# Gated one-hots in a top-k expert layer: one VectorE multiply per four tokens, or eight ScalarE copies with a per-partition scale

## The chip, the cores and the metric

The kernel runs on one core of one Trainium2 chip. The metric is device microseconds (us) of one execution, from the median of several runs. The engines are named as the profile names them: PE is TensorE (with PEld, its weight load), DVE is VectorE, ACT is ScalarE, POOL is GpSimd and SP is SyncE.

## What is computed

A two-layer network over 512 tokens of width 1024: a state-space mixer in layer 0, sliding-window attention in layer 1, and after each a "PEER" expert layer, which is where the change lies. Cut to what matters:

```python
def peer_ffn(x, norm_g, q_w, sub_keys, u, v):          # T = 512 tokens, 8 heads, 16 experts per head
    h = rmsnorm(x, norm_g).reshape(T, D)
    ...                                                # scores of 2 x 128 sub-keys, two top-16 lists,
    idx = jnp.take_along_axis(cand_i, best_pos, axis=-1)   # expert = i1 * 128 + i2, 16384 experts
    gate = jax.nn.softmax(best_s, axis=-1).astype(x.dtype)
    def block(inp):
        hb, ib, gb = inp
        a = jnp.einsum('nd,nhkd->nhk', hb, u[ib])
        w = gb * jax.nn.gelu(a, approximate=False)
        return jnp.einsum('nhk,nhkd->nd', w, v[ib])
```

## The kernel before

The first 128 tokens fetch their 128 expert rows each by indirect DMA (`gather_step`, L669). The other 384 tokens take another way: all 16384 experts are computed densely, and the gates are scattered into a dense matrix G of 16384 gates per token. G is made by matmuls of one-hots. For a token, the 128 chosen (head, rank) pairs lie on the partitions; `o[:, q, 0]` is the one-hot of i1, `o[:, q, 1]` that of i2, and `og` is the first one-hot times the gate. The gate is kept in two fp16 parts, a high one and the remainder, so `og` has two rows of 128 per token, and G of a token is the sum of two 128x128 matmuls of `o[:, q, 1]` with the parts of `og`.

**The stage.** In `peer` (L640) the loop over 128 blocks of experts (L982) does this in each step j: `lin` (L206) issues 24 matmuls, each 128x128 weights by 384 tokens, three for each of eight slices (L202 to L204); `next_w` (L154) has put a weight block's split ahead of it, ACT's `whi` copy (L169) and POOL's `wlo` subtraction in four quarters (L172), two blocks ahead; ACT takes the result through Gelu into `ga` (L993) and issues its store (L994); `gather(URATE)` (L995) does 1.17 steps of the gather on average, a DVE multiply (L678) and an indirect DMA (L695) each; and `self.step(BRATE)` (L996) takes background work out of a list.

**The order of the background work.** `bg` (L912) writes the list out by hand: a top-k of a head (T) costs 6.0, the decoding of the indices and gates of 128 tokens (D) some 11 in four items, a block of four tokens of G (G_) costs 1.5. A step adds 2.65 to a credit and takes items while the credit is above zero, so a step takes two blocks of G_ or one, and none for some steps after a T. Each block b is `onehot(b)` (L878) and, one item later, `gmm(b)` (L889): its eight matmuls (L898), the copy of the result to `gsz` by ACT (L899) and, after every fourth block, a store from ACT's queue (L902). Since `gmm` comes one item later, a step with two blocks issues in this order: `onehot(b)`, `gmm(b-1)`, `onehot(b+1)`, `gmm(b)`. All engines work in the order of issue.

```python
                    for b in range(32 * tt + lo, 32 * tt + hi):
                        items.append((1.5, lambda b=b: one(b)))
```

There are 96 blocks in each of the two layers. Tile buffers: `o` (its tile is named `early`) has 3, `og` 2, the score banks 2. The gates come to their place in `turn` (L861), once for each of three groups of 128 tokens: three PE transposes into a bank, then copies by ACT and DVE into `iT` (indices) and `gT` (gates), each value twice side by side so that DVE can read pairs.

Of the kernel before, what the change touches and what calls it, by code (L numbers as in the profile page):

```python
# [11 lines left out]
F32 = _mybir.dt.float32  # L12
# [4 lines left out]
AF = _mybir.ActivationFunctionType  # L17
OP = _mybir.AluOpType
AX = _mybir.AxisListType

P = 128
# [8 lines left out]
ND = NT - NG  # L30
# [4 lines left out]
QT = 4  # L35
GSCALE = 32768.0
F16 = _mybir.dt.float16
# [25 lines left out]
class Net:  # L63
# [54 lines left out]
    def plan(self):  # L118
        t, s = self.t, self.srcs
        w, off = t["wlin"], 0  # L120

        def lin(n):
            nonlocal off
            for _ in range(n):
                s.append(w[off])
                off += 1

        def peer(i):
            lin(16)
            for j in range(NBLK):  # L130
                s.append(t["ut"][i * NBLK + j])
            for j in range(NBLK):
                s.append(t["v"][i * NBLK + j])

        lin(66)
        peer(0)
        lin(8 + 21)
        peer(1)
        lin(8)
# [500 lines left out]
    def peer(self, L):  # L640
        nc, t, tc = self.nc, self.t, self.tc
        mm = nc.tensor.matmul
        vt = nc.vector
# [103 lines left out]
        with ExitStack() as ctx:  # L747
            mp = ctx.enter_context(tc.tile_pool(name="pm", bufs=2, reuse_waits="tile"))
            hp = ctx.enter_context(tc.tile_pool(name="ph", bufs=1, reuse_waits="tile"))
# [26 lines left out]
            pos = hp.tile([P, NTT, HEADS, TOPK], U32, name="pos")  # L776
            idx = hp.tile([P, 2, NTT, HEADS, TOPK], U32, name="idx")
            iT = hp.tile([P, ND, 2, 2], F16, name="iT")
            gT = hp.tile([P, ND, 2, 2], F16, name="gT")
            iota = hp.tile([P, P], F16, name="iota")  # L780
            vt.tensor_copy(iota, self.const[:, C_IOTA:C_IOTA + P])
            i16 = hp.tile([P, TOPK, QT], F16, name="i16")
# [30 lines left out]
            def fl(ap):  # L813
                return ap.rearrange("p a b -> p (a b)")
# [31 lines left out]
            def decode_e(tt):  # L846
                gt, fi = dec.pop(tt)
                sm = mp.tile([P, 2, HEADS], F32, name="sm")
                vt.tensor_reduce(sm[:, 0], gt, axis=AX.X, op=OP.add)
                vt.reciprocal(sm[:, 1], sm[:, 0])  # L850
                gk = mp.tile([P, TOPK, HEADS], F32, name="gk", bufs=1)
                vt.tensor_tensor(gk, gt.rearrange("p h k -> p k h"), sm[:, 1, None, :].to_broadcast([P, TOPK, HEADS]),
                                 op=OP.mult)
                if tt == 0:
                    ef = wg[:, 0]
                    vt.tensor_scalar(ef, fi[0], float(P), float(L * NBLK * P), op0=OP.mult, op1=OP.add)
                    vt.tensor_tensor(ef, ef, fi[1], op=OP.add)
                    vt.tensor_copy(eg, ef)
                    vt.tensor_copy(gate, fl(gk))

                def turn():  # L861
                    if tt == 0:
                        self.gi = 0
                        return
                    pt = self.bank(7)
                    for j, src in enumerate(fi + [fl(gk)]):
                        nc.tensor.transpose(pt[:, j * P:(j + 1) * P], src, self.ident)
                    ts = slice(tt * P - NG, (tt + 1) * P - NG)
                    two = lambda j: pt[:, j * P:(j + 1) * P, None].to_broadcast([P, P, 2])
                    for j in range(2):  # L870
                        nc.scalar.activation(iT[:, ts, j], two(j), AF.Copy)
                    nc.scalar.activation(gT[:, ts, 0], two(2), AF.Copy, scale=GSCALE)
                    vt.scalar_tensor_tensor(gT[:, ts, 1], two(2), GSCALE, gT[:, ts, 0], op0=OP.mult, op1=OP.subtract)
                return turn

            gs = {}
# [1 line left out]
            def onehot(b):  # L878
                o = mp.tile([P, QT, 2, P], F16, name="early", bufs=3)
                og = mp.tile([P, QT, 2, P], F16, name="og")  # L880
                ts = slice(QT * b - NG, QT * b - NG + QT)
                pairs = lambda ap: ap.rearrange("p t c (a d) -> p t c a d", d=2)
                alike = lambda ap: ap[:, ts, :, None, :].to_broadcast([P, QT, 2, P // 2, 2])
                vt.tensor_tensor(pairs(o), iota.rearrange("p (a d) -> p a d", d=2)[:, None, None].to_broadcast(  # L884
                    [P, QT, 2, P // 2, 2]), alike(iT), op=OP.is_equal)
                vt.tensor_tensor(pairs(og), pairs(o)[:, :, 0:1].to_broadcast([P, QT, 2, P // 2, 2]), alike(gT), op=OP.mult)  # L886
                return o, og

            def gmm(b, o):  # L889
# [22 lines left out]
            def bg():  # L912
# [12 lines left out]
                def G_(tt, lo, hi):  # L925
                    def one(b):
                        o = onehot(b)
                        return lambda: gmm(b, o)
                    for b in range(32 * tt + lo, 32 * tt + hi):
                        items.append((1.5, lambda b=b: one(b)))  # L930
# [24 lines left out]
            for c in range(2 * HEADS):  # L955
# [9 lines left out]
                q = hp.tile([P, NT], F32, name="ga", bufs=3)  # L965
# [40 lines left out]
        with vctx:  # L1006
            mp = vctx.enter_context(tc.tile_pool(name="pv", bufs=3, reuse_waits="tile"))
# [549 lines left out]
```

## Time and profile before

| | |
|---|---|
| runs shown | 3456.63, 3461.01, 3457.02 us; median 3457.02 |
| the profiled execution | 3453.39 us, its span 3451.6 us |
| PE, DVE, ACT, POOL busy in the span | 95%, 77%, 42%, 57% |
| mean granted TensorE clock | 0.983 of full speed |
| loop L982, first to last Gelu | layer 0: 644.65 to 1279.54 us; layer 1: 2205.21 to 2839.42 us |
| blocks of G within it | layer 0: 726.26 to 1189.31 us; layer 1: 2286.89 to 2747.86 us |

A row of a view gives start and duration in us, engine, line of the kernel, operation, tile written and tiles read, the shape, and in brackets how long the engine had been idle before and what ended that. Matmul durations overlap, so the pace of matmuls is read from their starts. "Busy" of an engine that waits for a port in the middle of an instruction counts as busy.

### The profile page before, as it was taken

The page shows a single profiled execution, that of the slowest core. Times are in us where ns is not written, and L with a number is a line of the kernel's source. Part 1 is how long each engine was busy: PE and PEld are TensorE (multiplying, and loading weights), DVE is VectorE, ACT ScalarE, POOL GpSimd, SP SyncE. Part 2 cuts the span into 40 slices and gives each one's busy share as a digit, 9 for nine tenths or more (in the row PEclk, how much of TensorE's full clock was granted, in tenths as well). Part 3 has the DMA queues.
Part 4 walks back from the last instruction along what each step waited for, and adds up shares of the span by engine and source line. Part 5 has one row for each costly group of instructions (what it writes and reads, how often), then busy time and mean ns, then how long its engine had stood idle before and what let it go on. Part 6 is the DMA issues. An engine that isn't in the chain of part 4 may idle for free.

```text
span 3451.6 us, 52253 instructions
## 1 busy us (share of the span) xinstructions
PE 3291.1 (95%) x18814; PEld 3022.6 (88%) x18814; DVE 2672.6 (77%) x4880; ACT 1455.2 (42%) x2198; POOL 1953.3 (57%) x2168
## 2 busy tenths in 40 slices
PE   8999999989999999999998999999999999999997
PEld 5777777989998989999996668989998989999996
DVE  7667667899998737878777865899988737877775
ACT  4433434444445533333334553444445533333334
POOL 5444545789888884322217226688888884322214
PEclk9999999999999999999999999999999999999998
DMA  3222212488888999999983112488888989999982
GB/s 119 85 77 70 74 62 75 151 280 309 309 312 303 330 310 358 358 336 346 337 286 107 45 59 89 138 278 308 316 309 297 334 304 356 353 346 339 339 304 85
DMA packets 357300, 827.50 MB, mean 240 GB/s; under 512 B 30000, under 2 KB 196528, under 8 KB 350896
## 3 DMA queue, kind: packets, MB, share of 16 engines
q1 hardware_dynamic: 235136, 448.59, 40.3%
q0 software_dynamic: 73728, 268.47, 21.1%
q10 hardware_dynamic: 48176, 107.10, 8.2%
q8 instruction: 147, 2.41, 0.3%
q14 instruction: 113, 0.93, 0.1%
HBM read 717.09 MB, written 106.95 MB: 239 GB/s over the span
## 4 chain that ended last, share of the span: by engine, by line
PE 58%; DVE 25%; POOL 7%; issue 5%; DMA 4%; ACT 1%; SPq 0%; POOLq 0%; DVEq 0%; ACTq 0%
PE bank L202 17%; PE bank L203 17%; PE bank L204 17%; POOL wlo L172 6%; DVE row L678 4%; DVE early L884 3%; DVE og L886 2%; DMA row<-u,eg 2%; POOL row L695 2%; DVE eq L840 1%; PE bank L898 1%; DMA wraw<-ut 1%; PE bank L971 1%; DVE eq L833 1%; DVE eq L837 1%
## 5 line engine op out<-in xcount | busy, mean ns | idle before, releaser
L172 POOL TENSOR_TENSOR wlo<-wraw,whi 128x256 fp32r<-128x256 f32 x1564 | 1256.1, 835 | 564.4 <-ACT whi L169 513.1
L169 ACT ACTIVATE whi<-wraw 128x1024 fp32r<-128x1024 f32 x647 | 685.5, 1061 | 740.5 <-issue 316.3
L695 POOL DMA_INDIRECT row<-v,eg x256 | 310.0, 1211 | 716.8 <-DVE yg L687 700.2
L204 PE MATMUL bank<-hhi,wlo 128*128 128x384 f32 x2048 | 699.8, 342 | 13.3 <-POOL wlo L172 13.2
L202 PE MATMUL bank<-hhi,whi 128*128 128x384 f32 x2048 | 708.6, 346 | 0.7 <-ACT whi L169 0.7
L203 PE MATMUL bank<-hlo,whi 128*128 128x384 f32 x2048 | 697.3, 340 | 0.0
L203 PE MATMUL bank<-vlo,whi 128*128 128x384 f32 x2032 | 684.1, 337 | 6.1 <-DVE vlo L744 6.0
L202 PE MATMUL bank<-vhi,whi 128*128 128x384 f32 x2032 | 684.8, 337 | 0.8 <-ACT vhi L742 0.8
L204 PE MATMUL bank<-vhi,wlo 128*128 128x384 f32 x2032 | 683.6, 336 | 0.0
L172 DVE TENSOR_TENSOR wlo<-wraw,whi 128x1024 fp32r<-128x1024 f32 x256 | 313.3, 1224 | 148.6 <-ACT whi L169 147.5
L204 PEld LDWEIGHTS bank<-hhi,wlo 128*128 128x128 f32 x2048 | 392.0, 191 | 20.0 <-POOL wlo L172 19.8
L202 PEld LDWEIGHTS bank<-hhi,whi 128*128 128x128 f32 x2048 | 393.3, 192 | 1.0 <-ACT whi L169 1.0
L203 PEld LDWEIGHTS bank<-hlo,whi 128*128 128x128 f32 x2048 | 392.8, 192 | 0.0
L203 PEld LDWEIGHTS bank<-vlo,whi 128*128 128x128 f32 x2032 | 382.6, 188 | 8.2 <-DVE vlo L744 8.2
L202 PEld LDWEIGHTS bank<-vhi,whi 128*128 128x128 f32 x2032 | 382.6, 188 | 2.0 <-ACT vhi L742 1.5
L204 PEld LDWEIGHTS bank<-vhi,wlo 128*128 128x128 f32 x2032 | 382.4, 188 | 0.3 <-POOL wlo L172 0.3
L678 DVE SCALAR_TENSOR_TENSOR row<-row,pair 128x1024 f32<-128x1024 f32 x256 | 305.6, 1212 | 88.1 <-DMA row<-u,eg 87.6
L687 DVE SCALAR_TENSOR_TENSOR yg<-row,wg,yg 128x1024 f32<-128x1024 f32 x254 | 328.0, 1291 | 35.9 <-DMA row<-v,eg 35.8
L202 PE MATMUL bank<-z,whi 128*128 128x512 f32 x728 | 322.0, 442 | 3.4 <-DVE sg L1137 3.4
L695 POOL DMA_INDIRECT row<-u,eg x256 | 278.5, 1088 | 50.4 <-issue 29.1
L993 ACT ACTIVATE ga<-bank 128x384 f32<-128x384 f32 x256 | 125.3, 490 | 418.0 <-PE bank L204 409.0
L203 PE MATMUL bank<-z,whi 128*128 128x512 f32 x728 | 291.1, 400 | 4.7 <-DVE z L262 4.7
(322 smaller groups left out, 4863.6 us busy)
## 6 DMA issues: line engine op xcount, KB each, us to landing
wraw<-ut SPq DMA_DIRECT2D x256, 512.0 KB
wraw<-v SPq DMA_DIRECT2D x256, 512.0 KB
wraw<-wlin SPq DMA_DIRECT2D x135, 512.0 KB
GA<-ga ACTq DMA_DIRECT2D x256, 192.0 KB
G<-gsz ACTq DMA_DIRECT2D x48, 1024.0 KB
gv<-G SPq DMA_DIRECT2D x96, 512.0 KB
gsz<-GA SPq DMA_DIRECT2D x256, 192.0 KB
PJ<-nf ACTq DMA_DIRECT2D x16, 256.0 KB
```

Source lines behind the costliest of these rows:

```text
L169: nc.scalar.activation(hi, r, AF.Copy)
L172: self.lo_eng.tensor_tensor(lo[:, q:q + n], r[:, q:q + n], hi.bitcast(F32)[:, q:q + n], op=OP.subtract)
L202: mm(out, whi, xhi, start=start, stop=False)
L203: mm(out, whi, xlo, start=False, stop=False)
L204: mm(out, wlo, xhi, start=False, stop=stop)
L678: vt.scalar_tensor_tensor(r, r, 1.0, self.pair, op0=OP.mult, op1=OP.mult, accum_out=wg[:, 0, j:j + 1])
L687: vt.scalar_tensor_tensor(yg, r, wg[:, 0, j:j + 1], yg, op0=OP.mult, op1=OP.add)
L695: nc.gpsimd.indirect_dma_start(out=got[i], out_offset=None, in_=t["u"] if i < NJ else t["v"].rearrange("a p d -> (a p) d"), in_offset=bass ...
L833: vt.tensor_tensor(eq.rearrange("p a (n q) -> p a n q", q=QT), fl(pb).rearrange("p (n q) -> p n q", q=QT)[:, None].to_broadcast([P, TOPK, ...
L884: vt.tensor_tensor(pairs(o), iota.rearrange("p (a d) -> p a d", d=2)[:, None, None].to_broadcast([P, QT, 2, P // 2, 2]), alike(iT), op=OP. ...
L886: vt.tensor_tensor(pairs(og), pairs(o)[:, :, 0:1].to_broadcast([P, QT, 2, P // 2, 2]), alike(gT), op=OP.mult)
L993: nc.scalar.activation(ga[:, NG:], ps[:, NG:], AF.Gelu)
```

## The change

`gT` holds one fp32 value per token and part instead of a pair of fp16 values. The DVE multiply that made a whole block of `og` (L886, 1024 values per partition) goes; in its place ACT makes eight copies of 128 values, one for each token and gate part, each from the plain one-hot `o[:, q, 0]`, with the gate as the scale per partition. In `turn`, ACT's pairwise copy of the high part becomes a plain copy into a new tile `gh`, DVE copies that to `gT` in fp32, and the remainder is computed on 128 values instead of 256.

```diff
-            gT = hp.tile([P, ND, 2, 2], F16, name="gT")
+            gT = hp.tile([P, ND, 2], F32, name="gT")
@@ turn
-                    nc.scalar.activation(gT[:, ts, 0], two(2), AF.Copy, scale=GSCALE)
-                    vt.scalar_tensor_tensor(gT[:, ts, 1], two(2), GSCALE, gT[:, ts, 0], op0=OP.mult, op1=OP.subtract)
+                    gh = mp.tile([P, P], F16, name="gh", bufs=1)
+                    nc.scalar.activation(gh, pt[:, 2 * P:3 * P], AF.Copy, scale=GSCALE)
+                    vt.tensor_copy(gT[:, ts, 0], gh)
+                    vt.scalar_tensor_tensor(gT[:, ts, 1], pt[:, 2 * P:3 * P], GSCALE, gh, op0=OP.mult, op1=OP.subtract)
@@ onehot
-                vt.tensor_tensor(pairs(og), pairs(o)[:, :, 0:1].to_broadcast([P, QT, 2, P // 2, 2]), alike(gT), op=OP.mult)
+                for q in range(QT):
+                    for j in range(2):
+                        nc.scalar.activation(og[:, q, j], o[:, q, 0], AF.Copy, scale=gT[:, ts.start + q, j:j + 1])
                 return o, og
```

## Rows read from the trace of the kernel before

**Rows 1.** The page's busy time, share of the span and instructions of each engine.

```profile
PE 3291.1 (95%) x18814; PEld 3022.6 (88%) x18814; DVE 2672.6 (77%) x4880; ACT 1455.2 (42%) x2198; POOL 1953.3 (57%) x2168
```

**Rows 2.** Windows: G stretches; length, busy PE, PEld, DVE, ACT, POOL, clock, DMA, GB/s.

```profile
726.26:1189.31 463.05, 428.12 (x2880) 415.55 (x2879) 428.55 (x739) 235.28 (x290) 402.74 (x459) 0.97 0.88 309
2286.89:2747.86 460.97, 427.87 (x2880) 415.73 (x2879) 415.50 (x739) 235.25 (x290) 404.99 (x459) 0.97 0.88 310
```

**Rows 3.** Waits, whole span: who waited for whom; us in total, times, longest.

```profile
PE bank L898 <- DVE og L886: 63.3, 35, 3.7
```

**Rows 4.** Timeline of ACT, a step without a block of G and its successor.

```profile
774.09 0.49 ACT L993 ACTIVATE ga<-bank 128x384 f32<-128x384 f32 x1 [1.18 <-PE bank L204]
...
778.25 0.49 ACT L993 ACTIVATE ga<-bank 128x384 f32<-128x384 f32 x1 [2.15 <-PE bank L204]
```

**Rows 5.** Timeline of ACT, a step with one block and one with two.

```profile
1101.47 0.49 ACT L993 ACTIVATE ga<-bank 128x384 f32<-128x384 f32 x1 [1.37 <-PE bank L204]
...
1102.37 1.08 ACT L899 ACTIVATE gsz<-bank 128x512 f32<-128x512 f32 x1 [0.40 <-ACT ga L993]
1103.48 0.33 ACTq L902 DMA_DIRECT2D G<-gsz  x1
1103.91 1.06 ACT L169 ACTIVATE whi<-wraw 128x1024 fp32r<-128x1024 f32 x1 [0.46 <-POOL wlo L172]
1106.15 0.49 ACT L993 ACTIVATE ga<-bank 128x384 f32<-128x384 f32 x1 [1.18 <-PE bank L204]
...
1107.17 2.00 ACT L899 ACTIVATE gsz<-bank 128x512 f32<-128x512 f32 x2
...
1111.28 0.49 ACT L993 ACTIVATE ga<-bank 128x384 f32<-128x384 f32 x1 [1.26 <-PE bank L204]
```

**Rows 6.** Line L886 among the groups of DVE: busy, mean ns, idle before.

```profile
L886 DVE TENSOR_TENSOR og<-early,gT 128x1024 f16<-128x1024 f16 x192 | 186.4, 971 | 56.7 <-PE bank L898 39.9 <-issue 0.5
```

**Rows 7.** Timeline of ACT: a 128-wide copy with scale per partition, and its successor.

```profile
519.33 0.40 ACT L256 ACTIVATE xf<-x,cols 128x128 f32<-128x128 f32 x1 [0.16 <-DVE x L596]
519.64 0.71 ACT L259 ACTIVATE z<-x,cols 128x512 fp32r<-128x512 f32 x1
```

**Rows 8.** Timeline of ACT: eight 128-wide activations from PSUM, bias per partition.

```profile
74.07 2.20 ACT L504 ACTIVATE L<-bank,nacs 128x128 f32<-128x128 f32 x8
```

**Rows 9.** Timelines of POOL and PE: a weight block split in quarters and its reader.

```profile
702.81 2.92 POOL L172 TENSOR_TENSOR wlo<-wraw,whi 128x256 fp32r<-128x256 f32 x4
...
703.60 0.44 PE L204 MATMUL bank<-hhi,wlo 128*128 128x384 f32 x1 [2.42 <-POOL wlo L172]
```

**Rows 10.** Timelines of DVE and PE at the first and last gap from 2.9 us up.

```profile
741.21 0.69 DVE L886 TENSOR_TENSOR og<-early,gT 128x1024 f16<-128x1024 f16 x1
...
741.96 0.70 PE L898 MATMUL bank<-og,early 128*128 128x128 f16 x8 [3.15 <-DVE og L886]
...
742.89 0.52 PE L203 MATMUL bank<-hlo,whi 128*128 128x384 f32 x1
...
745.77 0.35 PE L203 MATMUL bank<-hlo,whi 128*128 128x384 f32 x1
...
2621.87 1.01 PE L898 MATMUL bank<-og,early 128*128 128x128 f16 x8 [3.70 <-DVE og L886]
```

**Rows 11.** Timeline of PE around the start of the first step of rows 5.

```profile
1101.28 0.62 PE L898 MATMUL bank<-og,early 128*128 128x128 f16 x8
1101.71 0.42 PE L202 MATMUL bank<-hhi,whi 128*128 128x384 f32 x1
```

**Rows 12.** Window right after the first gap of rows 10, columns as in rows 2.

```profile
742.40:745.40 3.00, 3.00 (x13) 3.00 (x11) 2.79 (x6) 2.14 (x2) 0.03 (x1) 0.50 0.96 384
```

**Rows 13.** Timeline of PE: two shorter gaps close together, and a later matmul.

```profile
1058.42 0.61 PE L898 MATMUL bank<-og,early 128*128 128x128 f16 x8 [1.06 <-DVE og L886]
1061.73 1.01 PE L898 MATMUL bank<-og,early 128*128 128x128 f16 x8 [2.71 <-DVE og L886]
...
1062.97 0.52 PE L203 MATMUL bank<-hlo,whi 128*128 128x384 f32 x1
```

## The prediction

> **What bounds the kernel now.** I read each engine's share first [rows 1]: PE is busy 95%, DVE 77%, ACT 42%, so PE sets the pace and ACT looks half free. The change touches one stage, so next come the windows of the two stretches in which G is made [rows 2]: 924.0 us together (463.05 + 460.97), PE busy 93%, DVE 93% and 90%, ACT 51%. In the waits [rows 3] PE's matmuls wait 63.3 us for `og`, the largest wait of PE; DVE, nearly full, delivers late. That wait is what the change can win. What it can lose is in the order of the steps.
>
> I take the loop step as unit, from one Gelu (L993) to the next. Undisturbed it takes 4.16 us without a block [rows 4], 4.68 us with one `gmm` and 5.13 us with two [rows 5]. Following `bg`'s list with 2.65 credit per step and 1.5 per block through the code gives 88 steps in each stretch: 40 in which the last `gmm` needs an `og` issued in the same step (33 with two `onehot` and two `gmm`, 4 with two and one, 3 with one and two), 12 with one `onehot` and the `gmm` of an earlier block, 7 with an `onehot` alone, 7 with a `gmm` alone, 22 with neither. I call the 40 **dependent**. The other 48 at their undisturbed price are 19 x 4.68 + 29 x 4.16 = 209.6 us, so the dependent ones took 463.05 - 209.6 + 460.97 - 209.6 = 504.9 us, 6.31 each; undisturbed they would take about 5.13. The stalls of both stretches, some 94 us, lie all in them.
>
> **What goes.** DVE loses 192 multiplies, 186.4 us with their waits in mid-instruction [rows 6], 0.97 us on the mean; the shortest take 0.69. I book no gain for it by itself: in the dependent steps the new path replaces the old stall whole, and in the others DVE delays nothing today.
>
> **What comes: the price of a copy.** Each block puts eight 128-wide copies with a scale per partition on ACT. The same form, SBUF to SBUF, stands in another stage: 0.40 us, and the next instruction starts 0.31 us after it [rows 7]. So eight take 7 x 0.31 + 0.40 = 2.57 us to the end of the last, and 8 x 0.31 = 2.48 us of ACT's time. Bounds: 0.40 each, if these don't overlap; 0.275 each, as eight activations from PSUM go (2.20/8) [rows 8]. I take 0.31, the same operands and memories.
>
> The Trainium skill (ScalarE: Activation LUTs, Rules for kernel authors) speaks against the move: it gives multiplies to VectorE, up to about three times as fast per element in bf16. By that an `og` would cost at most 3 x 0.69 = 2.08 us on ACT, and the sum below would be some 32 us smaller (80 x 0.40); our row gives 2.48 / 0.69 = 3.6 times, so the trace agrees with its direction and goes further.
>
> **Where the copies lie.** ACT works in order. In a dependent step it does Gelu and the store's issue (0.90 us from L993 to the next instruction [rows 5]), then the copies of b, the `gsz` of b-1, the copies of b+1, the `gsz` of b, then `whi`. PE finishes `lin` and `gmm(b-1)`, and then needs `og(b)`, which ACT cannot begin before the Gelu of that same `lin`. DVE made its `og` while `lin` ran; ACT, behind the Gelu, can't. So a new wait lies on the path, and behind it on PE stands the whole next `lin`, on which the next Gelu waits.
>
> The matmul of a copy need not wait for all eight: PE started on a weight block 0.79 us after POOL had begun its four quarters of 2.92 us [rows 9], so waits go by pieces. Hence only the last matmul trails, 0.07 us (a `gmm` more in a step costs 0.52 us by the steps' difference, an eighth of that).
>
> Chain of a dependent step: 0.90 + 2.57 + 0.10 (handing over to PE: it began 0.06 us after DVE's `og` ended at 741.90 [rows 10], rounded up) + 0.07 + 4.44 (first matmul of `lin` at 1101.71 to the next Gelu at 1106.15 [rows 5, 11]) = 8.08 us. ACT's own work in it: 0.90 + 2 x 2.48 + 2.00 for two `gsz` + 0.22 (a G store's 0.43 every other step) + 1.06 for `whi` = 9.14 us [rows 5]. So even at full clock ACT sets 9.14.
>
> **The clock.** In the first 3.5 us of each such step PE does no more than two `gmm`, 0.62 us each [rows 11]. After each of the eight gaps of 2.9 us or more in the two stretches (the first 3.15, the last 3.70 [rows 10]) the granted clock fell to 0.50, that is 1.2 GHz [rows 12]: nine matmuls of `lin` took 2.88 us, 0.32 each, where 24 take 4.16, 0.17 each [rows 4, 10]. That lasted 2.88 us after the first gap and 3.15 on the mean of the eight, 1.59 at least, 4.78 at most; the loss is 46% of it, 1.45 us. With it the chain is 8.08 + 1.45 = **9.53 us**, longer than ACT's 9.14.
>
> **The other steps.** With one `onehot` and an older `gmm`, ACT needs 0.90 + 2.48 + 1.00 + 0.10 (a quarter of a G store) + 1.06 = 5.54 us where PE needs 4.68: 24 x 0.86 = 21 us. With an `onehot` alone 4.44 against 4.16: 14 x 0.28 = 4 us. Steps without copies stay. In `turn`, six times in all, ACT's copy and DVE's remainder halve in width and a DVE copy of 128 values comes, at most 0.69 us as the shortest multiply of 1024 has it: within 6 x 0.69 = 4 us either way, covered by `lin`, which runs while DVE prepares; without that cover those 4 us. I book zero. POOL, SP and the gathers keep their work per step and get more time for it: zero.
>
> **The sum.** 80 x (9.53 - 6.31) = 258, + 21 + 4 = **283 us**. Profiled execution 3453.4 (span 3451.6 and 1.8 around it) + 283 = 3736; the median of the runs shown lies 3.6 us above it, so **3740 us**. Without the clock's fall: 80 x (9.14 - 6.31) + 25 = 251, 3708. With copies at 0.40 ACT needs 10.58 a step: 80 x 4.27 + 24 x 1.58 + 14 x 1.00 = 394, 3851. At 0.275 and full clock, 8.58: 80 x 2.27 + 24 x 0.58 = 196, 3653.
>
> **Rivals.**
> - *Full clock.* The small matmuls between the copies keep the clock up; ACT's own 9.14 us decides: 3708. For it: each of the eight gaps was one piece, and here matmuls break it up. Against: two gaps of 1.06 and 2.71 us with eight small matmuls between them brought it down, 0.52 us for a matmul instead of 0.35 [rows 10, 13].
> - *Half clock through the whole `lin`.* The gap comes every 9 us, where today they are rare. 24 x 0.32 = 7.68 instead of 4.16: the step is 11.60, 80 x 5.29 + 25 = 448, 3905. Against: after each of today's gaps the clock was back within 4.8 us.
> - *DVE's relief decides; faster.* If the copies are ready when PE comes to them, the stalls go: 80 x (6.31 - 5.13) = 94 us less, 3363. For it: DVE is 93% busy and ACT 51% [rows 2]; and DVE's multiplies are drawn out by waits in mid-instruction (0.97 us on the mean, 0.69 bare [rows 6, 10]). It would decide if ACT had begun `og(b)` a step earlier, or from the point where eight copies take under 0.80 us (0.90 + 0.80 + 0.17 + 4.44 = 6.31); 2.57 us stand against it. The Trainium skill (GPSIMD Engine Reference, Specifications) says that GpSimd shares its SBUF interfaces with VectorE, with contention when a VectorE instruction has two SBUF inputs, as `og`'s multiply has; by that rule POOL too gets freer. The trace agrees in that the multiplies are drawn out, but POOL isn't late in these steps.
> - *It doesn't matter.* 96 x 2.48 = 238 us of copies fit arithmetically into ACT's 228 idle us of a stretch [rows 2], nearly. If ACT could work them off in the steps without blocks, the time would stay at 3457. The order forbids it: PE holds ACT's work back and ACT holds PE's.
>
> **Chances and range.** Forecast 0.55; full clock 0.25; half clock throughout 0.12; relief 0.05; no difference 0.03. About 0.2% (7 us) is what a measurement of this kernel can tell from no change: slower 0.92, same 0.03, faster 0.05. The range runs from 3645 to 3850: it takes in the forecast, the full clock and both bounds of a copy's price, and leaves out the half clock, the relief and no difference.
>
> **What would show it.** In the changed profile: `og` on ACT in groups of eight, 0.40 us each and 0.31 apart; PE's wait for `og` now put down to ACT, in some 80 steps; dependent steps near 9.5 us, the two stretches together near 1200 us instead of 924; ACT near 79% busy there (236 + 238 of some 600 us); DVE down by some 93 us in each; granted clock in the stretches well below 0.97; everything outside them unchanged. Copies further apart than 0.31 would put the price term wrong; a step of 9.14 us with the clock up, the clock term; dependent steps under 6.3 us, the whole forecast.

## The result and the profile after

The change makes the kernel slower: 3704.6 us against 3456.8, a ratio of 1.0715 (95% interval 1.0697 to 1.0733). The profiled execution took 3706.4 us, its span 3704.6. In the changed file the Gelu is L997, the copies are L890, the plain one-hot is L886, the matmuls of G are L902 and the copy of their result is L903.

First the page's busy time of the changed kernel [rows 1], then the windows of its two G stretches, from the same Gelu to the same Gelu as in [rows 2] and with the same columns:

```profile
PE 3455.0 (93%) x18814; PEld 3107.2 (84%) x18814; DVE 2431.4 (66%) x4694; ACT 1885.3 (51%) x3734; POOL 1901.0 (51%) x2168
```

```profile
722.23:1313.09 590.86, 515.60 (x2882) 463.28 (x2881) 302.19 (x653) 450.67 (x1058) 377.64 (x459) 0.90 0.70 244
2413.76:2999.27 585.51, 509.16 (x2882) 456.70 (x2881) 299.66 (x648) 450.34 (x1058) 377.17 (x457) 0.91 0.70 245
```

The stretches took 1176.4 us instead of 924.0, 252.4 more; the rest of the span is 2528.2 us against 2527.6. So the whole loss lies in the 176 steps that make G. ACT went from 51% to 77% of them, DVE from 91% to 51%, the clock from 0.97 to 0.90 and 0.91.

The waits and the group of the copies [rows 3, 6]:

```profile
DVE early L886 <- PE bank L902: 319.1, 105, 5.6
...
PE bank L902 <- ACT og L890: 96.9, 75, 2.6
```

```profile
L890 ACT ACTIVATE og<-early,gT 128x128 f16<-128x128 f16 x1536 | 467.2, 388 | 70.5 <-DVE early L886 34.8 <-ACT ga L997 27.0 <-DVE row L678 2.4
```

PE now waits for ACT's copies, 75 times, where it waited for DVE's multiply. DVE, relieved, waits 319.1 us for PE to release buffers. How a step goes shows best on ACT, in two dependent steps that follow one another [rows 5]:

```profile
1229.73 0.49 ACT L997 ACTIVATE ga<-bank 128x384 f32<-128x384 f32 x1 [1.55 <-PE bank L204]
1230.25 0.33 ACTq L998 DMA_DIRECT2D GA<-ga  x1
1230.62 2.44 ACT L890 ACTIVATE og<-early,gT 128x128 f16<-128x128 f16 x8 [0.40 <-ACT ga L997]
1232.97 1.04 ACT L903 ACTIVATE gsz<-bank 128x512 f32<-128x512 f32 x1
1233.80 2.41 ACT L890 ACTIVATE og<-early,gT 128x128 f16<-128x128 f16 x8
1236.11 1.04 ACT L903 ACTIVATE gsz<-bank 128x512 f32<-128x512 f32 x1
1236.95 1.06 ACT L169 ACTIVATE whi<-wraw 128x1024 fp32r<-128x1024 f32 x1
1237.90 0.47 ACT L997 ACTIVATE ga<-bank 128x384 f32<-128x384 f32 x1
1238.41 0.33 ACTq L998 DMA_DIRECT2D GA<-ga  x1
1238.78 2.45 ACT L890 ACTIVATE og<-early,gT 128x128 f16<-128x128 f16 x8 [0.40 <-DVE early L886]
...
1245.78 1.05 ACT L169 ACTIVATE whi<-wraw 128x1024 fp32r<-128x1024 f32 x1
1247.32 0.49 ACT L997 ACTIVATE ga<-bank 128x384 f32<-128x384 f32 x1 [0.48 <-PE bank L204]
```

The first of them is ACT from end to end: 8.17 us from Gelu to Gelu without a gap but the store's issue. The second took 9.42 us, and its Gelu waited for PE. What PE did in it, and the granted clock of the window that follows (columns as above):

```profile
1237.39 0.62 PE L902 MATMUL bank<-og,early 128*128 128x128 f16 x8
1239.23 2.26 PE L902 MATMUL bank<-og,early 128*128 128x128 f16 x8 [1.22 <-ACT og L890]
1241.30 0.42 PE L202 MATMUL bank<-hhi,whi 128*128 128x384 f32 x1
...
1242.44 0.53 PE L204 MATMUL bank<-hhi,wlo 128*128 128x384 f32 x1
1242.76 0.53 PE L202 MATMUL bank<-hhi,whi 128*128 128x384 f32 x1
```

```profile
1242.00:1244.00 2.00, 2.00 (x8) 2.00 (x7) 1.39 (x3) 1.60 (x6) 0.48 (x1) 0.51 0.78 164
```

The eight matmuls of a block follow the eight copies one by one, 0.29 us apart (2.26 us for eight that otherwise take 0.62), and then `lin` runs for about 3 us at 1.2 GHz, a matmul every 0.32 us. In the step before it PE did the same behind a gap of 0.92 us, and `lin` ran at the full clock:

```profile
1231.08 2.26 PE L902 MATMUL bank<-og,early 128*128 128x128 f16 x8 [0.92 <-ACT og L890]
```

```profile
1233.20:1237.40 4.20, 4.20 (x26) 4.04 (x25) 1.92 (x4) 4.20 (x11) 0.00 (x0) 1.00 0.56 226
```

So two things alternate: steps in which ACT is full, and steps in which the chain Gelu, copies, last matmul, `lin` at a lowered clock is longer. A slow stretch shows in PE's timeline as matmuls of `lin` that start 0.32 us apart instead of 0.17. Of the 80 dependent steps 49 have one, 3.3 us long on the mean; they take 9.00 to 10.59 us, 9.60 on the mean. The other 31 have none; they take 7.83 to 8.95 us, 8.37 on the mean. The mean of all 80 is 9.13 us.

### The profile page after: what moved, and what is told of

It is laid out like the page before. It is cut to its first block, busy times and chain, and to the rows that moved or that the text cites. A ratio compares the mean times of both kernels' runs of the same rounds, so it can differ in the third digit from the quotient of the medians.

```text
span 3704.6 us, 53697 instructions
## 1 busy us (share of the span) xinstructions
PE 3455.0 (93%) x18814; PEld 3107.2 (84%) x18814; DVE 2431.4 (66%) x4694; ACT 1885.3 (51%) x3734; POOL 1901.0 (51%) x2168
## 4 chain that ended last, share of the span: by engine, by line
PE 60%; DVE 13%; ACT 9%; POOL 6%; issue 6%; DMA 4%; ACTq 1%; SPq 0%; POOLq 0%; DVEq 0%
PE bank L202 18%; PE bank L203 18%; PE bank L204 18%; ACT og L890 6%; POOL wlo L172 5%; POOL row L695 1%; PE bank L902 1%; DVE row L678 1%; DMA row<-u,eg 1%; DVE eq L840 1%; ACT ga L997 1%; ACT gsz L903 1%; DMA gsz<-GA 1%; DMA wraw<-ut 1%; PE bank L975 1%
## 5 line engine op out<-in xcount | busy, mean ns | idle before, releaser
L172 POOL TENSOR_TENSOR wlo<-wraw,whi 128x256 fp32r<-128x256 f32 x1564 | 1228.7, 819 | 864.9 <-ACT whi L169 815.2
L202 PE MATMUL bank<-hhi,whi 128*128 128x384 f32 x2048 | 737.9, 360 | 3.0 <-ACT whi L169 3.0
L204 PE MATMUL bank<-hhi,wlo 128*128 128x384 f32 x2048 | 724.5, 354 | 15.3 <-POOL wlo L172 15.0
L203 PE MATMUL bank<-hlo,whi 128*128 128x384 f32 x2048 | 723.6, 353 | 0.0
L890 ACT ACTIVATE og<-early,gT 128x128 f16<-128x128 f16 x1536 | 467.2, 388 | 70.5 <-DVE early L886 34.8
L202 PEld LDWEIGHTS bank<-hhi,whi 128*128 128x128 f32 x2048 | 414.0, 202 | 19.1 <-issue 15.4
L203 PEld LDWEIGHTS bank<-hlo,whi 128*128 128x128 f32 x2048 | 413.8, 202 | 0.0
L886 DVE TENSOR_TENSOR early<-iota,iT 128x1024 f16<-128x1024 f16 x192 | 162.7, 857 | 319.1 <-PE bank L902 319.1
L902 PE MATMUL bank<-og,early 128*128 128x128 f16 x1536 | 219.3, 223 | 150.7 <-ACT og L890 96.9
L202 PE MATMUL bank<-z,whi 128*128 128x512 f32 x728 | 320.7, 440 | 3.4 <-DVE sg L1141 3.4
```

What stands on the lines that cost most here:

```text
L172: self.lo_eng.tensor_tensor(lo[:, q:q + n], r[:, q:q + n], hi.bitcast(F32)[:, q:q + n], op=OP.subtract)
L202: mm(out, whi, xhi, start=start, stop=False)
L203: mm(out, whi, xlo, start=False, stop=False)
L204: mm(out, wlo, xhi, start=False, stop=stop)
L890: nc.scalar.activation(og[:, q, j], o[:, q, 0], AF.Copy, scale=gT[:, ts.start + q, j:j + 1])
L902: mm(ps[:, q * P:(q + 1) * P], o[0][:, q, 1], o[1][:, q, j], start=(j == 0), stop=(j == 1))
```

## The experiments

All times are medians; each kernel was compared with the kernel before on the same chip, which stood at 3455 to 3462 us. "Step" is the mean of the 80 dependent steps (the same steps of the list in each run, from Gelu to Gelu; where the matmuls come an item later, those of a block have moved on to a later step), "G" the sum of both stretches. Both are from the profiled execution, which lies at most 10 us from the median (e7's is the fastest of its ten runs, e10's the slowest of its eleven).

| kernel | us | ratio to before (95%) | step, us | G, us |
|---|---|---|---|---|
| before | 3456.8 | | 6.31 | 924 |
| the change | 3704.6 | 1.0715 (1.0697 to 1.0733) | 9.13 | 1176 |
| e1: change, matmuls an item later | 3614.7 | 1.0459 (1.0435 to 1.0483) | 8.18 | 1087 |
| e3: before, copies as load alone | 3622.1 | 1.0483 (1.0462 to 1.0505) | 8.36 | 1088 |
| e4: change, one wide copy | 3525.6 | 1.0200 (1.0180 to 1.0220) | 7.09 | 997 |
| e5: change, PE kept at work | 3668.2 | 1.0616 (1.0589 to 1.0642) | 8.59 | 1133 |
| e2: change, half the copies | 3528.6 | 1.0192 (1.0167 to 1.0217) | 7.07 | 995 |
| e9: change, no scale operand | 3582.7 | 1.0357 (1.0341 to 1.0373) | 7.77 | 1052 |
| e6: before, matmuls an item later | 3430.7 | 0.9903 (0.9883 to 0.9924) | 5.83 | 897 |
| e7: half the copies, an item later | 3449.8 | 0.9968 (0.9955 to 0.9982) | 6.19 | 915 |
| e8: a quarter of the copies, an item later | 3422.1 | 0.9895 (0.9878 to 0.9912) | 5.80 | 891 |
| e10: e6 with the step's order turned | 3452.9 | 0.9983 (0.9973 to 0.9994) | 5.97 | 920 |

The theory was the coupling of PE and ACT through the order of the step. Its rivals were that ACT's load alone does it, and that the clock is what makes the steps long.

### e1: the copies a step ahead

```diff
-                og = mp.tile([P, QT, 2, P], F16, name="og")
+                og = mp.tile([P, QT, 2, P], F16, name="og", bufs=3)
-                        items.append((1.5, lambda b=b: one(b)))
+                        items.append((1.5, lambda b=b: one(b), 2))
```

> The changed kernel with the matmuls of a block issued two items after its one-hots instead of one, and a third buffer for the gated one-hots, so that no step needs copies made in the same step. The copies themselves stay, 16 in a step with two blocks. Coupling theory (a dependent step is long because PE waits for copies that stand behind the Gelu of the same step, and the clock falls in that wait): the wait goes, ACT's own 8.2 to 8.4 us stays; 80 x (8.3 - 9.13) = 66 us less than the changed kernel, about 3640. Load theory (ACT is simply full and PE's wait only follows from that): 3705 as before this edit, within 15 us. If the copies were harmless once they are early: 3460 or less.

Measured 3614.7, 90 us under the change, 159 over the kernel before. The third buffer and the lead were changed together; with two buffers the lead has no room. PE's waits in this run:

```profile
PE bank L902 <- ACT gsz L903: 124.3, 78, 4.0
...
PE bank L902 <- ACT og L890: 9.6, 4, 2.6
```

The wait for the copies is gone (96.9 to 9.6 us), and PE waits for a score bank instead, which ACT empties late because it is full. Load alone therefore does not explain 9.13 us, but ACT's load holds the larger part of the loss. The step is shorter than I had priced it (8.18 against 8.3), and the gain larger (90 us against 66), since other steps shrank too, by 13 us in all. The clock rose only part of the way (columns as above):

```profile
724.19:1269.88 545.69, 462.49 (x2909) 439.57 (x2908) 302.34 (x647) 444.04 (x1058) 381.86 (x457) 0.94 0.75 263
2368.43:2910.00 541.57, 460.14 (x2909) 438.43 (x2908) 302.11 (x651) 444.60 (x1058) 385.27 (x459) 0.94 0.76 266
```

In 33 of the 80 steps `lin` still has a slow stretch. But these take 8.17 us on the mean and the others 8.19, and in none of the 80 does the next Gelu wait for PE: beside a full ACT the lowered clock shows no cost.

### e3: the load without the need

```diff
                 vt.tensor_tensor(pairs(og), ..., alike(gT), op=OP.mult)
+                dm = mp.tile([P, QT, 2, P], F16, name="dm", bufs=1)
+                for q in range(QT):
+                    for j in range(2):
+                        nc.scalar.activation(dm[:, q, j], o[:, q, 0], AF.Copy, scale=self.cols[:, j:j + 1])
```

> The kernel before, in which DVE makes the gated one-hots, with eight copies per block added on ACT that write a tile nobody reads. Same load on ACT, none of it on PE's path except through ACT's order. Load theory: as long as the changed kernel, 3690 to 3720. Coupling theory: ACT's 8.2 to 8.4 us per step with two blocks, no long wait of PE for a gated one-hot, so shorter than the changed kernel by 40 to 70 us, about 3650. If ACT's idle time took the copies in: 3457.

Measured 3622.1: 167 us over the kernel before without any use made of the copies, and 82 under the change, more than the 40 to 70 expected. It agrees with e1 from the other side, and its largest wait of PE is again that for the bank:

```profile
PE bank L902 <- ACT gsz L903: 110.0, 70, 3.6
```

### e4: the need without the load

```diff
-                for q in range(QT):
-                    for j in range(2):
-                        nc.scalar.activation(og[:, q, j], o[:, q, 0], AF.Copy, scale=gT[:, ts.start + q, j:j + 1])
+                nc.scalar.activation(og, o[:, :, 0:1].to_broadcast([P, QT, 2, P]), AF.Copy)
```

> The changed kernel with the eight copies of a block made as one copy of 1024 values, without the gates as scale (the gates are left out of G, so the output is another). The wait behind the Gelu stays, ACT's load falls from 2.4 to about 1 us per block. Coupling theory: chain 0.90 + 1.06 + 0.10 + 0.52 + 4.44 = 7.0 us in a dependent step against 6.31 before the change: 80 x 0.7 = 55 us over the kernel before, about 3510. Load theory: ACT needs 6.2 us in such a step, no more than before: 3457 or, with DVE freer, down to 3420.

Measured 3525.6, 70 us over the kernel before. A step, on ACT and PE:

```profile
1100.70 0.49 ACT L995 ACTIVATE ga<-bank 128x384 f32<-128x384 f32 x1 [0.89 <-PE bank L204]
...
1101.59 1.06 ACT L888 ACTIVATE og<-early 128x1024 f16<-128x1024 f16 x1 [0.40 <-ACT ga L995]
...
1107.56 0.49 ACT L995 ACTIVATE ga<-bank 128x384 f32<-128x384 f32 x1 [1.30 <-PE bank L204]
```

```profile
1102.70 0.61 PE L900 MATMUL bank<-og,early 128*128 128x128 f16 x8 [1.58 <-ACT og L888]
```

ACT has idle time in the step (its next Gelu waits 1.30 us for PE), and yet the step takes 6.86 us, as most of the 80 do to within 0.15, against the 7.0 of the chain. The wait behind the Gelu is a cost of its own, without a full ACT and with the clock at 0.98 to 0.99 in the stretches. Its 70 us are for a copy of 1.06 us; eight narrow ones last longer. They are 15 us more than expected, since 11 of the 80 steps take 7.15 to 9.62 us, seven of them with `lin` slow.

### e5: the clock

```diff
+            FIRST = [0, 2, 5, 7, 9, 13, ...]
+            seen = []
             def gmm(b, o):
+                again = 5 if len(seen) in FIRST else 1
+                seen.append(b)
...
+                for _ in range(again):
                     for q in range(4):
                         for j in range(2):
                             mm(ps[:, q * P:(q + 1) * P], o[0][:, q, 1], o[1][:, q, j], start=(j == 0), stop=(j == 1))
```

> The changed kernel in which the first of the two groups of eight matmuls in a dependent step is done five times over, in 72 of the 80 dependent steps: 2.1 us more of matmuls, laid where PE waits for the copies. Clock theory (the half-speed stretch after that wait makes the step longer): the clock stays up, steps near ACT's 8.2 us: 72 x 0.8 = 58 us less than the changed kernel, about 3645. If the clock costs nothing because ACT is the longer arm: 3705 within 10 us. If the added matmuls lie on the path: 72 x 2.1 = 150 us more, 3855.

Measured 3668.2, 36 us under the change although 36 x 4 x 8 matmuls per layer were added. The two stretches:

```profile
724.58:1289.05 564.47, 532.04 (x4034) 489.38 (x4033) 301.39 (x646) 448.24 (x1059) 378.91 (x457) 0.98 0.73 254
2393.17:2961.42 568.25, 535.92 (x4032) 492.41 (x4031) 297.74 (x651) 448.40 (x1060) 378.85 (x458) 0.97 0.73 253
```

The clock came back to 0.98 and 0.97. Of the 80 dependent steps 12 still have a slow stretch of `lin`, where 49 had one, and its time fell from 161 us to 36; seven of the 12 are among the eight steps that got no added matmuls. The steps are now mostly ACT's: 8.17 us without a G store, 8.85 with one. In the steps with a single `onehot` and two `gmm`, where ACT is not full, the bare chain shows: 7.84 us. So keeping the clock up is worth these 36 us of the 248, 44 in the two stretches, and possibly more, since 12 slow steps are left. It is less than the 58 us expected, which presumed 8.2 us for all 72 steps: with the G stores the 68 steps at full pace take 8.43 us on the mean, and the eight without added matmuls grew from 8.53 to 9.38.

### e2 and e9: the price of the copies

e2 leaves the low part of the gate to DVE (512 values per block); e9 puts a constant in the place of the gate.

```diff
...
                 for q in range(QT):
-                    for j in range(2):
-                        nc.scalar.activation(og[:, q, j], o[:, q, 0], AF.Copy, scale=gT[:, ts.start + q, j:j + 1])
+                    nc.scalar.activation(og[:, q, 0], o[:, q, 0], AF.Copy, scale=gT[:, ts.start + q:ts.start + q + 1])
+                one = lambda ap, c: ap.rearrange("p t c (a d) -> p t c a d", d=2)[:, :, c]
+                vt.tensor_tensor(one(og, 1), one(o, 0), gL[:, ts, None, :].to_broadcast([P, QT, P // 2, 2]), op=OP.mult)
```

> The changed kernel with only the high part of each gate copied by ACT (four copies per block) and the low part multiplied by DVE (512 values per block). ACT in a step with two blocks: 8.2 - 8 x 0.29 = 5.9 us. Coupling theory: chain 0.90 + 4 x 0.29 + 0.10 + 0.10 + 0.07 + 4.44 = 6.8 us, clock up, since the wait is halved: 80 x (6.8 - 6.31) = 39 us over the kernel before, about 3495. Load theory: ACT is no longer full, so 3457 or less. Half of the whole effect, if it went in proportion: 3580.

Measured 3528.6. The step is 6.75 us where nothing else is late, the 6.8 of the chain; the mean is 7.07, since ten steps, which come after top-k work, take 8.3 to 11.2. In all ten `lin` has a slow stretch (the shortest take 8.31, 1.56 us over the 6.75); in some DVE's plain one-hot comes late too, and ACT stands in front of it for up to 2.41 us. The sum was right by its step and short by these.

```diff
-                        nc.scalar.activation(og[:, q, j], o[:, q, 0], AF.Copy, scale=gT[:, ts.start + q, j:j + 1])
+                        nc.scalar.activation(og[:, q, j], o[:, q, 0], AF.Copy, scale=1.0 + j)
```

> The changed kernel with the eight copies of a block scaled by a constant in place of the gate per partition (the gates are left out of G, so the output is another). It prices the operand. If the operand per partition costs 0.09 us a copy, as the 0.40 and 0.31 us of the kernel before suggest for 128-wide activations with and without one, copies come 0.20 us apart: ACT's full step falls from 8.17 to 6.7 us, the chain is 0.90 + 1.71 + 0.17 + 4.44 = 7.2 us, the clock mostly up: 80 x (7.2 - 6.31) + 15 = 86 us over the kernel before, about 3545. If the operand is free and the 0.29 us are the instruction itself: 3705.

Measured 3582.7. The source row of the copy (shortest, median and longest in ns), and behind it eight in a row, from ACT's timeline:

```profile
L890 ACT ACTIVATE og<-early x1536: 279/293/327, 727.4 to 2872.5; 128x128 f16<-128x128 f16 x192
```

```profile
1111.21 1.70 ACT L890 ACTIVATE og<-early 128x128 f16<-128x128 f16 x8 [0.40 <-issue]
```

293 ns instead of 387, and (1.70 - 0.29)/7 = 0.20 us apart instead of 0.29: the operand per partition costs 0.09 us a copy. Undisturbed steps take 7.1 us, the chain's 7.2. In 26 of the 80 `lin` has a slow stretch, and most of these take 8.68, 1.56 us more; the expectation had the clock mostly up; hence 3583 and not 3545.

### e6, e7, e8, e10: is there a version that beats both?

e6 is the edit of e1 made to the kernel before. e7 is e2 with it. e8 is e6 in which ACT gets one token of four (two copies) and DVE the other three:

```diff
...
+                n, t0 = QT - 1, ts.start
+                for j in range(2):
+                    nc.scalar.activation(og[:, n, j], o[:, n, 0], AF.Copy, scale=gF[:, t0 // QT, j:j + 1])
+                vt.tensor_tensor(pairs(og)[:, :n], pairs(o)[:, :n, 0:1].to_broadcast([P, n, 2, P // 2, 2]),
+                                 gT[:, t0:t0 + n, :, None, :].to_broadcast([P, n, 2, P // 2, 2]), op=OP.mult)
```

> The kernel before with the matmuls of a block issued two items after its one-hots and a third buffer for the gated ones. Coupling theory: the stalls of the kernel before (94 us in dependent steps) come from the same need within the step; with DVE a step ahead most go: 3365 to 3410. If DVE is simply full there (93% busy): 3440 to 3457.

> Both edits: four copies per block on ACT, the low part on DVE, and the matmuls two items after the one-hots. ACT 5.9 us in a step with two blocks, PE 5.13, DVE relieved of half a multiply per block. Coupling theory: no wait within the step, ACT's 5.9 sets it, against 6.31 before: 72 x 0.4 = 29 us under the kernel before, about 3428. If an even split beats DVE alone with the same order, it is below the run with the old multiply and this order; if ACT's queue is the dearer place, above it.

> The kernel before with matmuls two items after the one-hots, and of the four tokens of a block one given to ACT (two copies) and three left to DVE's multiply (768 values). ACT in a step with two blocks: 8.17 - 12 x 0.29 = 4.7 us, under PE's 5.13. If DVE's fullness is what is left of the stalls, a quarter of a multiply less helps: 3405 to 3425, under the run with the whole multiply (3431). If ACT's order is dear even for two copies: 3431 to 3450.

e6 is 1.0% faster than the kernel before (3430.7), between its two expectations. PE's wait for `og` fell from 63.3 us [rows 3]; DVE is as full as it was, or fuller [rows 2]:

```profile
PE bank L898 <- DVE og L886: 38.5, 29, 3.2
```

```profile
724.56:1174.31 449.75, 424.39 (x2877) 409.95 (x2876) 438.98 (x735) 233.18 (x290) 413.69 (x456) 0.98 0.90 317
2276.89:2724.36 447.47, 424.25 (x2872) 410.65 (x2871) 433.99 (x735) 234.27 (x289) 406.40 (x456) 0.98 0.90 318
```

DVE at 98% and 97% is the likely rest of the stalls, but neither e8 nor e10 shows it. e7, expected at 3428, measured 3449.8 and is slower than e6 (its step 6.19 against 5.83): even four copies put ACT's 5.9 us where PE needs 5.13. e8, with two, measured 3422.1, within the 3405 to 3425 expected of a lighter DVE, ratio 0.9895 against e6's 0.9903; the intervals overlap, so that two copies help beyond the order is not shown. e6 and e8 both beat the kernel before and the change.

```diff
-                gather(URATE)
                 self.step(BRATE)
+                gather(URATE)
```

> The kernel before with matmuls two items after the one-hots, and in each loop step the background items issued ahead of the gather's multiplies, so that on DVE the one-hots no longer stand behind products that wait for rows. If the remaining stalls come from that order: 3400 to 3420. If DVE is simply full: 3431 within 7 us. If the gather falls behind: above 3440.

e10, e6 with this exchange, gained nothing: 3452.9, slower than e6 and hardly faster than before. In its profile PE waits 34.8 us for POOL's `wlo`, where it waits 18.6 in e6; whether that is the cause stays open.

## Why the prediction was right, and by how much its size was off

Sign, place and mechanism held; 3705 lies within the range, 35 us under the predicted 3740. By its steps:

- **What bounds, and where.** The 176 steps of G and nothing else: shown by the windows. That DVE's relief brings nothing by itself held too: DVE fell from 91% to 51% and the time rose; POOL got freer too, 754.8 us of work in the stretches instead of 807.7. The rival of the relief (3363) fell with e1, where DVE is as free, the copies are ready a step earlier and the time is still 159 us over the kernel before, and with e4, where it is 70 over.
- **The price of a copy.** 0.31 us apart was forecast, 0.29 measured, and eight in 2.45 us against 2.57. The row of the nearest form [rows 7] was the right one. Eight copies hold ACT's queue for some 2.33 us (1230.62 to 1232.97 and 1233.80 to 1236.11), 3.4 times the 0.69 us of DVE's bare multiply: nearer to the 3.6 that the prediction took from its row than to the ratio of three beside it.
- **The wait behind the Gelu.** Shown alone by e4 (70 us), and by e1, which takes it away (90 us) and with it what the lowered clock costs, though not all of the clock's fall. That the matmuls follow their copies piece by piece was right; the chain at full clock was 7.84 us, forecast 8.08.
- **The term that was off** is the dependent step, "the chain is 8.08 + 1.45 = 9.53 us, longer than ACT's 9.14": measured 9.13. I let the clock fall in each of the 80. It fell in 49, and these took 9.60 us, close to the 9.53; the fall costs 1.56 us (9.42 against the 7.86 of steps with two `onehot`, one `gmm` and no slow stretch), close to the forecast 1.45. In the other 31 the step is 8.37 us, not even the 9.14 of ACT's arm. ACT's full step is 8.17 us, some 8.85 with a G store: I had added the copies at 0.31 us and `gsz` and `whi` at their pace from [rows 5], but in an unbroken queue eight copies take 2.33 us, and `gsz` and `whi` 0.83 and 0.95 (1236.11 to 1236.95 to 1237.90). 31 x 1.16 = 36 us too much and 49 x 0.07 = 3 too little, together some 32. Why the clock fell in these 49 and not in the 31 stays open.
- **The other steps.** With one `onehot` and an older `gmm`: 5.15 us, forecast 5.54, 9 us too much in all. With an `onehot` alone: 5.47, forecast 4.44, 14 us too little. Ten of the 14 took 4.20 us, but the four that open a long run of blocks took 6.86 to 10.55: there ACT stood for 3.06 to 6.76 us in front of a one-hot that DVE, late from the top-k, had not made, as here:

```profile
728.28 2.45 ACT L890 ACTIVATE og<-early,gT 128x128 f16<-128x128 f16 x8 [5.55 <-DVE early L886]
```

  I had looked for waits of PE on ACT and missed ACT's own on DVE. With `gmm` alone: 4.42, forecast 4.68, 4 us too much. Together 32 + 9 - 14 + 4 = 31 us, about the miss of 30 (283 against 253 of span).
- **The rivals.** "Full clock" gave 3708, almost the measured time, and was wrong all the same: the clock fell in 49 steps, and e5, where it mostly stays up, is at 3668. Its 9.14 us per step met the mean of 8.37 and 9.60 by chance. "Half clock through the whole `lin`" did not come: the slow stretch took 3.3 us on the mean and 5.1 at most, where a whole `lin` at that pace would take 7.68. "It doesn't matter" was wrong by e3: copies that nobody needs already cost 167 us.

The parts of the loss, by the runs: 159 us stay when the copies come early enough (ACT's load and what it delays), 90 go with the wait; keeping the clock up without taking the wait away wins back 36 by e5. That the parts add up is not shown separately, since each run also shifts the others.

## What to carry to other kernels

An engine that is half idle over the whole span can still be the wrong place for work: count what it must do in one turn of the loop, in its order, and see what it stands behind. Work for which the next engine waits in the same turn must not be queued behind an instruction that itself waits for that engine; a buffer more and a turn's lead took 90 of 248 us back here, and made the kernel before 1.0% faster. For the same 1024 values eight narrow copies with an operand per partition cost 2.45 us, eight without it 1.70 (e9) and one wide copy without it 1.06 (e4): the number of instructions and the operand of each were the price, not the number of values.

## What the runs showed of the hardware that I had not expected

- The granted clock fell to 0.51 after a wait in which PE was idle for no more than 1.22 us at once and then did eight small matmuls, 0.29 us apart. The gap alone does not tell: of the 25 dependent steps whose longest gap was 0.92 us, 7 had the slow stretch and 18 not. In the kernel before, the clock had fallen after all eight gaps of 2.9 us and more in the stretches [rows 10] and after one of 2.05, but not after one of 2.87 (`lin` behind it kept its pace); the window, columns as above, follows the gap of 2.05. In e4, with gaps of 1.58 us and the small matmuls close together, it mostly stayed (0.98 and 0.99).

```profile
798.70 0.62 PE L898 MATMUL bank<-og,early 128*128 128x128 f16 x8 [2.87 <-DVE og L886]
2693.83 0.62 PE L898 MATMUL bank<-og,early 128*128 128x128 f16 x8 [2.05 <-DVE og L886]
```

```profile
2695.00:2697.00 2.00, 2.00 (x8) 2.00 (x7) 1.99 (x4) 1.42 (x2) 1.24 (x2) 0.50 1.05 411
```

- Matmuls that compute the same result again, laid into that wait, made the kernel 36 us faster.
- An operand per partition lengthens a 128-wide copy on ACT from 293 to 387 ns, and the pace of such copies from 0.20 to 0.29 us.
